# Eight of 31 convolution taps moved to ScalarE and GpSimd, and the product order and operand buffers of a seven-product FFN changed

## The chip, the cores and the metric

The kernel runs on one core of one Trainium2 chip, as one launch. The metric is the device time of that launch in microseconds. The engines are named as the profile names them: PE is TensorE, DVE is VectorE, ACT is ScalarE, POOL is GpSimd, SP is SyncE, whose queue issues most DMAs.

## What is computed

One layer of an encoder over 1024 tokens of width 1024, all in float32: a mixer of two branches, then a SwiGLU network (FFN) of width 2816, each with a residual, and a last RMS norm.

```python
h = rmsnorm(x, norm_mix)
a_val, a_gate, u, v, g_a, g_b = split(h @ w_in)          # six times 1024 columns
c = a_val * sigmoid(a_gate)
c = depthwise_conv(c, conv_w, conv_b)                    # width 31, centred, along the tokens
y_a = silu(layernorm(c, conv_ln_g, conv_ln_b)) @ w_conv_out
y_b = spatial_gating(u, v) @ w_sgu_out                   # 128x128 position mixing per chunk and group
x = x + (sigmoid(g_a + gb_a) * y_a + sigmoid(g_b + gb_b) * y_b) @ w_o
h2 = rmsnorm(x, norm_ffn)
x = x + (silu(h2 @ w_ffn_gate) * (h2 @ w_ffn_up)) @ w_ffn_down
return rmsnorm(x, norm_final)
```

## The kernel before

**Operands in two parts.** Every float32 matrix operand is split into a high part (rounded to fp32r by ACT, L84) and a low part (the rest, by DVE, L85), and a product is three matmuls: high by high, high by low, low by high. A matmul has 128 rows by 512 columns.

**Mixer.** Channels lie on partitions, tokens on the free axis, so a channel's 1024 tokens are one row. The program runs as a list of jobs of 48 matmuls, each with one 128-column block of weights: for each of eight channel blocks j a gate job (pg) and a value job (pv), from which c_j is made; between them the v products and the mixing; then eight pu jobs, then eight pairs pb and py, then eight pga jobs. The two parts of a job's weights lie in the pool tag wh with four buffers, that is two jobs' weights: the split for a job can begin when the job two places ahead of it has ended on PE, and must be done when the job just ahead of it ends.

**Convolution.** Each channel block's 31 taps are done on DVE beside those jobs: the centre tap writes conv_j with the bias (L212), the other 30 are each one scalar_tensor_tensor, conv_j = c_j shifted, times a weight per channel, plus conv_j (L218). They stand in the queue bg; pump(n) emits the next n of them after a job, and what is left is emitted after the last py job. The sum over the channel blocks (conv_sum, L396) goes to PE as conv_mean behind the first pga job.

**FFN.** After two plain rows f = 0 and 1, ten iterations take two rows of 128 columns each. The product of a 2x2 block of weights (two rows by two halves of the inputs) with a 2x2 block of activations is made by seven products in place of eight, for the gate (call g) and for the up matrix (call u). The names p1 to p7 stand here for the product of weight operand w1 to w7 with its activation operand: a product is 12 matmuls. The activation operands (y11, y21, y22, t1 to t4, four tiles each) are made once and stay in the pool act. The weight operands are made for every call by w_operands: four sums on DVE and seven splits, all into the four buffers of wh. Products land in two PSUM tiles of two banks each, pa (b1 and b2) and pb (b3), and are read by ACT or DVE between products: s1 = copy of b1 (L654), s2 (L656), s3 (L660), then the four results.

**Who sets the order.** The code gives each engine's work and the tiles; a scheduler at build time sets the order on each engine, and an engine runs its list strictly in that order. It orders a product into pa behind a read of the other bank of pa. Pools: act has 42 buffers of 4 KB per partition, tmp two, and a tile can be written when the last user of its buffer is done.

## Time and profile before

| what | value |
|---|---|
| median of 2 runs | 1554.85 us (1554.05 to 1555.65) |
| profiled execution, its own time | 1553.29 us |
| its span, first to last instruction | 1551.5 us |
| PE busy, share of the span | 1508.7 us, 97% |
| DVE busy | 925.7 us, 60% |
| ACT busy | 419.8 us, 27% |
| POOL busy | 68.0 us, 4% |
| granted TensorE clock, mean | 0.998 of full speed |

PE is the engine to explain. Matmuls overlap, so a PE that is shown as busy is not a PE at its rate: the number of matmuls in a stretch tells how near it is. Shares of the other engines are means over stages that differ much; a stage is read by its own windows.

### The profile page before, as it was taken

To read this page: it belongs to the slowest core of one execution; us is meant where nothing else is said; L and a number is where in the kernel's file an instruction comes from. 1 tells how busy PE (TensorE), PEld (TensorE's weight loads), DVE (VectorE), ACT (ScalarE), POOL (GpSimd) and SP (SyncE) were. 2 spreads that over 40 slices of the span, in tenths; PEclk is the share of its full clock that TensorE was granted. 3 is DMA by queue.
4 is the path that set the end of the run, shared out by engine and by line. 5 is a ranking of instruction groups with operands and counts; after the bars stand their busy time and mean duration, and the time that the engine had idled before them with its cause. 6 is when DMAs were issued, how large, how long until landed. Compare 5 with 4: busy or idle time off the path is not lost.

```text
span 1551.5 us, 16509 instructions
## 1 busy us (share of the span) xinstructions
PE 1508.7 (97%) x6728; PEld 1228.4 (79%) x6728; DVE 925.7 (60%) x1115; ACT 419.8 (27%) x603; POOL 68.0 (4%) x116
## 2 busy tenths in 40 slices
PE   6999999999999999999999999999999999999997
PEld 6888888888888888888888777777777777887885
DVE  5889799498999526434523755555555555444412
ACT  6220101121111115612323422222223223333301
POOL 1000100000000000110010000000000000000000
PEclk9999999999999999999999999999999999999999
DMA  4240011111222122461611212122222224663502
GB/s 191 71 137 14 10 33 41 54 42 55 62 74 81 55 96 82 138 229 41 230 64 59 95 68 67 69 68 82 82 76 74 82 86 160 220 199 103 183 1 81
DMA packets 43036, 141.73 MB, mean 91 GB/s; under 512 B 4785, under 2 KB 4785, under 8 KB 42961
## 3 DMA queue, kind: packets, MB, share of 16 engines
q1 hardware_dynamic: 32256, 101.73, 20.3%
q0 software_dynamic: 10704, 38.96, 6.9%
q8 instruction: 52, 0.85, 0.2%
q14 instruction: 24, 0.19, 0.0%
HBM read 112.36 MB, written 28.31 MB: 91 GB/s over the span
## 4 chain that ended last, share of the span: by engine, by line
PE 96%; ACT 2%; DVE 1%; issue 0%; DMA 0%; POOL 0%; POOLq 0%; SPq 0%; ACTq 0%; DVEq 0%
PE fd L494 15%; PE pa_g L640 9%; PE pa_u L640 9%; PE pga L110 6%; PE po L494 6%; PE py L110 6%; PE pb L110 6%; PE pu L110 6%; PE pco L110 6%; PE pv L110 5%; PE pg L110 5%; PE pb_g L640 4%; PE pb_u L640 3%; PE v L298 2%; PE v L300 2%; PE v L299 2%
## 5 line engine op out<-in xcount | busy, mean ns | idle before, releaser
L218 DVE SCALAR_TENSOR_TENSOR conv<-c,vec,conv 128x1021 f32<-128x1021 f32 (+14 forms) x240 | 301.1, 1272 | 4.4
L494 PE MATMUL fd<-wh_d,ff 128*128 128x512 f32 x704 | 198.9, 389 | 2.0 <-ACT ff L84 2.0
L494 PEld LDWEIGHTS fd<-wh_d,ff 128*128 128x128 f32 x704 | 132.0, 188 | 29.9 <-ACT ff L84 2.5
L84 ACT CAST wh_in<-ws_in 128x1024 fp32r<-128x1024 f32 x40 | 42.2, 1054 | 303.3 <-PE pg L110 77.5
L494 PE MATMUL fd<-wl_d,ff 128*128 128x512 f32 x352 | 118.7, 389 | 0.0
L640 PE MATMUL pa_g<-t,w_g 128*128 128x512 f32 x360 | 89.8, 398 | 0.0
L640 PE MATMUL pa_u<-t,w_u 128*128 128x512 f32 x360 | 88.6, 395 | 0.4 <-DVE s_u L660 0.4
L640 PEld LDWEIGHTS pa_g<-t,w_g 128*128 128x128 f32 x360 | 65.3, 188 | 20.7 <-ACT fa L677 3.1
L640 PEld LDWEIGHTS pa_u<-t,w_u 128*128 128x128 f32 x360 | 66.0, 188 | 18.5 <-DVE fa L688 3.0
L494 PEld LDWEIGHTS fd<-wl_d,ff 128*128 128x128 f32 x352 | 66.1, 188 | 13.8
L110 PE MATMUL pg<-hT,wh_in 128*128 128x512 f32 (+1 forms) x272 | 74.1, 383 | 2.6 <-DVE hT L181 2.0
L85 DVE TENSOR_TENSOR wl_in<-ws_in,wh_in 128x1024 fp32r<-128x1024 f32 x40 | 48.8, 1219 | 41.2 <-ACT wh_in L84 41.1
L110 PE MATMUL pv<-hT,wh_in 128*128 128x512 f32 (+1 forms) x272 | 71.0, 377 | 0.0
L110 PE MATMUL pga<-hT,wh_in 128*128 128x512 f32 x256 | 69.4, 393 | 0.0
L494 PE MATMUL po<-wh_o,mT 128*128 128x512 f32 x256 | 69.1, 390 | 0.0
L110 PE MATMUL pco<-sT,wh_co 128*128 128x512 f32 x256 | 68.4, 389 | 0.0
L110 PE MATMUL pu<-hT,wh_in 128*128 128x512 f32 x256 | 68.4, 389 | 0.0
L110 PE MATMUL pb<-hT,wh_in 128*128 128x512 f32 x256 | 68.4, 389 | 0.0
L110 PE MATMUL py<-gT,wh_so 128*128 128x512 f32 x256 | 68.4, 389 | 0.0
L85 DVE TENSOR_TENSOR wl_d<-ws_d,wh_d 128x1024 fp32r<-128x1024 f32 x32 | 39.1, 1225 | 45.9 <-ACT wh_d L84 45.8
L640 PE MATMUL pa_g<-y,w_g 128*128 128x512 f32 x240 | 61.4, 399 | 2.6 <-ACT w_g L84 2.3
L110 PEld LDWEIGHTS pg<-hT,wh_in 128*128 128x128 f32 x272 | 50.5, 188 | 14.3 <-DVE hT L181 3.3
(216 smaller groups left out, 2654.0 us busy)
## 6 DMA issues: line engine op xcount, KB each, us to landing
ws_in<-in_w_in SPq DMA_DIRECT2D x40, 512.0 KB, 3.7
ws_d<-in_w_down SPq DMA_DIRECT2D x32, 512.0 KB, 4.0
ws_g<-in_w_gate SPq DMA_DIRECT2D x22, 512.0 KB, 3.6
ws_u<-in_w_up SPq DMA_DIRECT2D x22, 512.0 KB, 4.4
ff_d<-fa POOLq DMA_DIRECT2D x22, 512.0 KB, 4.0
ffr<-ff_d SPq DMA_DIRECT2D x44, 256.0 KB, 3.7
x<-in_x SPq DMA_DIRECT2D x16, 512.0 KB, 6.5
ws_v<-in_w_v SPq DMA_DIRECT2D x8, 512.0 KB, 3.7
```

Source lines behind the costliest of these rows:

```text
L84: nc.scalar.copy(hi, src)
L85: nc.vector.tensor_sub(lo, src, hi.bitcast(F32))
L110: nc.tensor.matmul(p[:, h * H + lo_t:h * H + hi_t], wt[:, sl], a[part][h][j][:, i, lo_t:hi_t], start=(k == 0 and wt is hi and part == 0), ...
L218: nc.vector.scalar_tensor_tensor(o[:, a:b], c[:, a + d:b + d], vcol(V_CW, j * TAPS + t), o[:, a:b], ALU.mult, ALU.add)
L298: nc.tensor.matmul(p[:, i2, :], lh, whi, start=(k == 0), stop=False)
L299: nc.tensor.matmul(p[:, i2, :], lh, wlo, start=False, stop=False)
L300: nc.tensor.matmul(p[:, i2, :], ll, whi, start=False, stop=(k == KT - 1))
L494: nc.tensor.matmul(p[c], l[:, sl], r[:, c * H:(c + 1) * H], start=(start and l is lh and r is wh), stop=(stop and l is ll))
L640: nc.tensor.matmul(p, w[n][:, q, sl], a[i][:, r, :], start=(start and i == 0 and m == 0), stop=(i == 3 and m == 2), skip_group_check=True)
```

## The change

**Convolution.** Of the 30 taps beside the centre, the eight nearest to it (SIDE) leave DVE. ACT multiplies the shifted c_j by the tap's weight: the first into a tile side_j, the other seven into tiles tap_j. POOL adds those seven to side_j (L241), and DVE adds side_j to conv_j at the end (join). The side taps stand in bg between DVE's taps, one for every two.

**FFN.** The products run in the order p1, p2, p6, p5, p7, p3, p4; before, p1, p6, p2, p7, p5, p4, p3. w1 is made with the opposite sign, so that results are one difference each. The reads of PSUM between products are three copies on ACT and three differences on DVE per call, with the last result read straight from PSUM; before, one copy and five differences. The operands w3, w6 and w7 lie in the pool act, so that wh's four buffers hold w1, w2, w4 and w5 alone. The tile u moves from act to tmp.

**Memory.** The pool act has 45 buffers in place of 42, and the scratch for DMA descriptors of POOL's queue is set to 4096 bytes.

```diff
@@ -35,7 +35,7 @@
     nc = tc.nc
 
     const = ctx.enter_context(tc.tile_pool(name="const", bufs=1))
-    act = ctx.enter_context(tc.tile_pool(name="act", bufs=42))
+    act = ctx.enter_context(tc.tile_pool(name="act", bufs=45))
     tmp = ctx.enter_context(tc.tile_pool(name="tmp", bufs=2))
     wp = ctx.enter_context(tc.tile_pool(name="wp", bufs=2))
     small = ctx.enter_context(tc.tile_pool(name="small", bufs=4))
@@ -206,22 +206,49 @@
     hT = pairs()
     conv = [None] * KT
 
+    SIDE = [PAD - 1, PAD + 1, PAD - 2, PAD + 2, PAD - 3, PAD + 3, PAD - 4, PAD + 4]
+
     def queue_conv(j, c):
+        side = [None]
+
         def center():
             conv[j] = A(f"conv_{j}")
             nc.vector.tensor_scalar(conv[j], c, vcol(V_CW, j * TAPS + PAD), vcol(V_CB, j),
                                     ALU.mult, ALU.add)
 
+        def cols(t):
+            d = t - PAD
+            a, b = max(0, -d), S - max(0, d)
+            return slice(a, b), slice(a + d, b + d)
+
         def tap(t):
-            o, d = conv[j], t - PAD
-            a, b = max(0, -d), S - max(0, d)
-            nc.vector.scalar_tensor_tensor(o[:, a:b], c[:, a + d:b + d],
-                                           vcol(V_CW, j * TAPS + t), o[:, a:b],
+            to, of = cols(t)
+            o = conv[j]
+            nc.vector.scalar_tensor_tensor(o[:, to], c[:, of], vcol(V_CW, j * TAPS + t), o[:, to],
                                            ALU.mult, ALU.add)
+
+        def side_tap(n, t):
+
+            to, of = cols(t)
+            if n == 0:
+                side[0] = A(f"side_{j}")
+                nc.gpsimd.memset(side[0][:, 0:1], 0.0)
+                nc.scalar.activation(side[0][:, to], c[:, of], AF.Copy,
+                                     scale=vcol(V_CW, j * TAPS + t))
+                return
+            m = A(f"tap_{j}_{t}")
+            nc.scalar.activation(m[:, to], c[:, of], AF.Copy, scale=vcol(V_CW, j * TAPS + t))
+            nc.gpsimd.tensor_tensor(side[0][:, to], side[0][:, to], m[:, to], op=ALU.add)
+
+        def join():
+            nc.vector.tensor_add(conv[j], conv[j], side[0])
         bg.append(center)
-        for t in range(TAPS):
-            if t != PAD:
-                bg.append(lambda t=t: tap(t))
+        rest = [t for t in range(TAPS) if t != PAD and t not in SIDE]
+        for n, t in enumerate(rest):
+            if n % 2 == 0 and n // 2 < len(SIDE):
+                bg.append(lambda n=n // 2, t=SIDE[n // 2]: side_tap(n, t))
+            bg.append(lambda t=t: tap(t))
+        bg.append(join)
 
     def glu_out(j, sg, pg, pv):
         c = A(f"c_{j}")
@@ -609,6 +636,7 @@
 
     def w_operands(src, f, name):
 
+
         r0, r1 = w_raw(src[f], f"{name}{f}"), w_raw(src[f + 1], f"{name}{f + 1}")
         x11, x12, x21, x22 = r0[:, :H], r0[:, H:], r1[:, :H], r1[:, H:]
         sa, sb = two(f"sa_{name}{f}"), two(f"sb_{name}{f}")
@@ -616,20 +644,28 @@
         out = {}
 
         def put(n, s):
-            o = wp.tile([P, 2, H], F32R, tag="wh", name=f"w{n}_{name}{f}", bufs=4)
-            split(s, o[:, 0, :], o[:, 1, :])
+            if n in (6, 7, 3):
+                o = two(f"w{n}_{name}{f}", F32R)
+            else:
+                o = wp.tile([P, 2, H], F32R, tag="wh", name=f"w{n}_{name}{f}", bufs=4)
+            hi, lo = o[:, 0, :], o[:, 1, :]
+            if n == 1:
+                nc.scalar.activation(hi, s, AF.Copy, scale=-1.0)
+                nc.vector.scalar_tensor_tensor(lo, s, -1.0, hi.bitcast(F32), ALU.mult, ALU.subtract)
+            else:
+                split(s, hi, lo)
             out[n] = o
         put(1, x11)
+        put(2, x12)
         nc.vector.tensor_add(sp, x21, x22)
         nc.vector.tensor_add(sq, x11, sp)
         put(6, sq)
-        put(2, x12)
+        put(5, sp)
         nc.vector.tensor_add(sr, x11, x21)
         put(7, sr)
-        put(5, sp)
-        put(4, x22)
         nc.vector.tensor_add(sz, x12, sq)
         put(3, sz)
+        put(4, x22)
         return out
 
     def block(p, w, n, start):
@@ -647,46 +683,45 @@
 
         pa, pb = PS(f"pa_{name}", (P, 2, H)), PS(f"pb_{name}", (P, 2, H))
         b1, b2, b3 = pa[:, 0, :], pa[:, 1, :], pb[:, 0, :]
-        s12 = two(f"s12_{name}")
-        s3_ = A(f"s3_{name}", F32, (P, H))
-        s1, s2, s3 = s12[:, 0, :], s12[:, 1, :], s3_
+        s12, s5 = two(f"s12_{name}"), A(f"s5_{name}", F32, (P, H))
+        s1, s2 = s12[:, 0, :], s12[:, 1, :]
         block(b1, w, 1, True)
         nc.scalar.copy(s1, b1)
-        block(b2, w, 6, True)
-        nc.vector.tensor_sub(s2, b2, s1)
-        block(b1, w, 2, False)
-        c11(b1)
-        block(b2, w, 7, False)
-        nc.vector.tensor_sub(s3, b2, s1)
+        block(b2, w, 2, True)
+        c11(lambda o: nc.vector.tensor_sub(o, b2, s1))
+        block(b1, w, 6, False)
+        nc.scalar.copy(s2, b1)
         block(b3, w, 5, True)
-        c22(lambda o: nc.vector.tensor_sub(o, s3, b3))
-        block(b2, w, 4, False)
-        c21(lambda o: nc.vector.tensor_sub(o, b2, s1))
+        nc.scalar.copy(s5, b3)
+        block(b1, w, 7, False)
+        c22(lambda o: nc.vector.tensor_sub(o, b1, s5))
         block(b3, w, 3, False)
         c12(lambda o: nc.vector.tensor_sub(o, b3, s2))
+        block(b1, w, 4, False)
+        c21(b1)
 
     def ffn_in(f, wg, next_w):
         a = [two(f"fa_{f + n}") for n in range(2)]
 
         def gate_block(n, h):
-            def put(sub):
-                sub(a[n][:, h, :])
+            def put(add):
+                add(a[n][:, h, :])
                 nc.scalar.activation(a[n][:, h, :], a[n][:, h, :], AF.Silu)
             return put
-        blocks(wg, f"g{f}",
-               lambda b: nc.scalar.activation(a[0][:, 0, :], b, AF.Silu),
-               gate_block(1, 0), gate_block(1, 1), gate_block(0, 1))
+        blocks(wg, f"g{f}", gate_block(0, 0),
+               lambda b: nc.scalar.activation(a[1][:, 0, :], b, AF.Silu),
+               gate_block(1, 1), gate_block(0, 1))
         wu = w_operands(w_up, f, "u")
-        u = two(f"u_{f}")
+        u = T(f"u_{f}", (P, 2, H))
 
         def up_block(n, h, i):
-            def put(sub):
-                sub(u[:, i, :])
+            def put(add):
+                add(u[:, i, :])
                 nc.vector.tensor_mul(a[n][:, h, :], a[n][:, h, :], u[:, i, :])
             return put
-        blocks(wu, f"u{f}",
-               lambda b: nc.vector.tensor_mul(a[0][:, 0, :], a[0][:, 0, :], b),
-               up_block(1, 0, 0), up_block(1, 1, 1), up_block(0, 1, 0))
+        blocks(wu, f"u{f}", up_block(0, 0, 0),
+               lambda b: nc.vector.tensor_mul(a[1][:, 0, :], a[1][:, 0, :], b),
+               up_block(1, 1, 1), up_block(0, 1, 0))
         wn = next_w()
         for n in range(2):
             nc.gpsimd.dma_start(ff_d[f + n], a[n].rearrange("p a b -> p (a b)"))
@@ -811,7 +846,8 @@
     }
     arrays = {f"in_{k}": _np.ascontiguousarray(v) for k, v in arrays.items()}
 
-    nc = _bacc.Bacc("TRN2", target_bir_lowering=False, num_devices=1)
+    nc = _bacc.Bacc("TRN2", target_bir_lowering=False, num_devices=1,
+                     dynamic_dma_scratch_size=4096)
     args = [nc.dram_tensor(k, v.shape, _mybir.dt.from_np(v.dtype), kind="ExternalInput").ap()
             for k, v in arrays.items()]
     for i, (shape, dtype) in enumerate(_OUTS):
```

The order on PE is the same in both kernels up to the first of the seven-product calls. Within a call it changes. On PE, call g for rows 8 and 9, from the end of p1 on (y11, y21 and t2 are the activation operands of p1, p2 and p6; t1 with w5 is p5, which fills in), before:

```order
L640 MATMUL pa_g8_6544<-y11_3_5106,w1_g8_6515 128x512 x3
L640 MATMUL pb_g8_6545<-t1_0_5609,w5_g8_6530 128x512 x2
L640 MATMUL pa_g8_6544<-t2_0_5603,w6_g8_6520 128x512 x3
L640 MATMUL pa_g8_6544<-t2_1_5621,w6_g8_6520 128x512 x3
L640 MATMUL pa_g8_6544<-t2_2_5688,w6_g8_6520 128x512 x3
L640 MATMUL pa_g8_6544<-t2_3_5706,w6_g8_6520 128x512 x3
L640 MATMUL pb_g8_6545<-t1_0_5609,w5_g8_6530 128x512
L640 MATMUL pb_g8_6545<-t1_1_5627,w5_g8_6530 128x512 x3
L640 MATMUL pa_g8_6544<-y21_0_5181,w2_g8_6523 128x512 x3
```

and now:

```order
L676 MATMUL pa_g8_6680<-y11_3_5242,w1_g8_6651 128x512 x3
L676 MATMUL pb_g8_6681<-t1_0_5745,w5_g8_6662 128x512 x3
L676 MATMUL pb_g8_6681<-t1_1_5763,w5_g8_6662 128x512
L676 MATMUL pa_g8_6680<-y21_0_5317,w2_g8_6654 128x512 x3
L676 MATMUL pa_g8_6680<-y21_1_5321,w2_g8_6654 128x512 x3
L676 MATMUL pa_g8_6680<-y21_2_5335,w2_g8_6654 128x512 x3
L676 MATMUL pa_g8_6680<-y21_3_5339,w2_g8_6654 128x512 x3
L676 MATMUL pb_g8_6681<-t1_1_5763,w5_g8_6662 128x512 x2
L676 MATMUL pb_g8_6681<-t1_2_5830,w5_g8_6662 128x512 x2
L676 MATMUL pa_g8_6680<-t2_0_5739,w6_g8_6659 128x512 x3
```

Behind p1 stood two matmuls of p5 and then p6; now four of p5 stand there, then p2, four more of p5, then p6.

On ACT, around the same call: L84 makes high parts, s12 is the tile of s1 and s2 (and s5 holds p5), fa are the FFN's activations. Before:

```order
L84 CAST w1_g8_6515<-ws_g8_6509 128x512 [waits DMAHW2_49,DVE_49,PE_49]
L84 CAST w6_g8_6520<-sa_g8_6513 128x512 [waits DVE_49,PE_49,Activation_49]
L84 CAST w2_g8_6523<-ws_g8_6509 128x512 [waits PE_49,Activation_49]
L84 CAST w7_g8_6527<-sb_g8_6514 128x512 [waits DVE_49,PE_49,Activation_49]
L84 CAST w5_g8_6530<-sa_g8_6513 128x512 [waits PE_49,Activation_49]
L654 COPY s12_g8_6546<-pa_g8_6544 128x512
L84 CAST w4_g8_6533<-ws_g9_6511 128x512 [waits DMAHW3_49,DVE_49,PE_49]
L84 CAST w3_g8_6537<-sb_g8_6514 128x512 [waits DVE_49,PE_49,Activation_49]
L677 ACTIVATE fa_8_6542<-pa_g8_6544 128x512 [waits DMASW1_49,DVE_49]
```

and now:

```order
L84 CAST w5_g8_6662<-sa_g8_6649 128x512 [waits DVE_49,Activation_49]
L84 CAST w6_g8_6659<-sa_g8_6649 128x512 [waits DMASW0_49,DVE_49]
L84 CAST w7_g8_6666<-sb_g8_6650 128x512 [waits DVE_49]
L84 CAST w3_g8_6670<-sb_g8_6650 128x512 [waits DVE_49]
L84 CAST w4_g8_6673<-ws_g9_6647 128x512 [waits DMAHW1_49,PE_49,Activation_49]
L689 COPY s12_g8_6682<-pa_g8_6680 128x512 [waits PE_49]
L653 ACTIVATE w1_u8_6784<-ws_u8_6778 128x512 [waits DMAHW2_49,Activation_49]
L84 CAST w2_u8_6787<-ws_u8_6778 128x512 [waits PE_49,Activation_49]
L709 ACTIVATE fa_8_6678<-fa_8_6678 128x512 [waits DVE_49]
L693 COPY s12_g8_6682<-pa_g8_6680 128x512 [waits PE_49]
L695 COPY s5_g8_6683<-pb_g8_6681 128x512 [waits PE_49]
L709 ACTIVATE fa_9_6679<-fa_9_6679 128x512 [waits DVE_49]
```

All seven casts of call g8 now stand ahead of its first copy of PSUM (its w1 and w2 still earlier, in the call before), and the casts that follow are of call u8; before, five stood ahead of it, each behind the release of a wh buffer, and two behind it.

On ACT in the mixer, from the end of the job pu_6 on (wh_in32 are the weights of pb_0, wh_so0 those of py_0, side_5 and tap_5 the side taps of channel block 5). Before:

```order
L84 CAST wh_in32_2445<-ws_in32_2443 128x1024 [waits DMAHW0_49,PE_49,Activation_49]
L84 CAST gT0_0_3_2499<-mixed_6_1522 128x512 [waits DVE_49]
L84 CAST gT0_1_3_2503<-mixed_6_1522 128x512
L84 CAST wh_so0_2515<-ws_so0_2513 128x1024 [waits DMAHW1_49,PE_49,Activation_49]
L84 CAST gT0_0_3_2499<-mixed_7_1533 128x512 [waits DVE_49]
L84 CAST gT0_1_3_2503<-mixed_7_1533 128x512
L84 CAST wh_in33_2596<-ws_in33_2594 128x1024 [waits DMAHW2_49,PE_49,Activation_49]
```

and now:

```order
L84 CAST wh_in32_2525<-ws_in32_2523 128x1024 [waits DMAHW0_49,PE_49,Activation_49]
L84 CAST gT0_0_3_2579<-mixed_6_1562 128x512 [waits DVE_49,Activation_49]
L84 CAST gT0_1_3_2583<-mixed_6_1562 128x512 [waits Pool_49]
L236 ACTIVATE side_5_2655<-c_5_1827,vec_83 128x1023 [waits Pool_49]
L240 ACTIVATE tap_5_16_2733<-c_5_1827,vec_83 128x1023 [waits Activation_49]
L240 ACTIVATE tap_5_13_2738<-c_5_1827,vec_83 128x1022 [waits DVE_49]
L240 ACTIVATE tap_5_17_2743<-c_5_1827,vec_83 128x1022 [waits Pool_49]
L240 ACTIVATE tap_5_12_2805<-c_5_1827,vec_83 128x1021 [waits Pool_49]
L240 ACTIVATE tap_5_18_2810<-c_5_1827,vec_83 128x1021 [waits Pool_49]
L240 ACTIVATE tap_5_11_2872<-c_5_1827,vec_83 128x1020 [waits Pool_49]
L84 CAST wh_so0_2594<-ws_so0_2592 128x1024 [waits DMAHW1_49,PE_49]
L240 ACTIVATE tap_5_19_2877<-c_5_1827,vec_83 128x1020 [waits Pool_49]
```

Seven multiplications now stand between two casts of weights, five of them with a wait for POOL.

## Rows read from the trace of the kernel before

**Rows 1.** Two windows: PE, PEld, DVE, ACT, POOL busy us (count), clock, DMA, GB/s.

```profile
400.00:500.00 100.00, 100.00 (x443) 82.81 (x442) 99.94 (x86) 15.52 (x15) 2.37 (x5) 1.00 0.21 69
...
900.00:1000.00 100.00, 95.67 (x402) 73.22 (x401) 52.70 (x83) 28.57 (x49) 2.13 (x4) 1.00 0.22 74
```

**Rows 2.** Chain that ended last, in order of time: start, us, piece.

```profile
302.36 87.04 PE pu L110 x384
389.40 10.88 PE pb L110 x48
...
574.37 1.72 PE conv_mean L403 x4
...
880.61 2.73 PE pa_g L640 x12
...
922.64 2.51 PE pa_g L640 x11
...
964.48 2.51 PE pa_g L640 x11
...
1299.45 119.69 PE fd L494 x528
```

**Rows 3.** Timeline of call g, rows 6 and 7: start, us, instruction, idle before.

```profile
967.06 0.62 ACT L84 CAST w_g<-sa_g 128x512 fp32r<-128x512 f32 x1 [1.88 <-PE pa_g L640]
...
967.59 0.58 ACT L654 COPY s_g<-pa_g 128x512 f32<-128x512 f32 x1
...
967.73 0.30 PEld L640 LDWEIGHTS pb_g<-t,w_g 128*128 128x128 f32 x2 [1.19 <-ACT w_g L84]
...
968.30 2.95 PE L640 MATMUL pa_g<-t,w_g 128*128 128x512 f32 x12
...
971.36 0.69 DVE L656 TENSOR_TENSOR s_g<-pa_g,s_g 128x512 f32<-128x512 f32 x1 [2.95 <-PE pa_g L640]
...
972.11 3.02 PE L640 MATMUL pa_g<-y,w_g 128*128 128x512 f32 x12
...
980.18 3.02 PE L640 MATMUL pa_g<-t,w_g 128*128 128x512 f32 x12
```

**Rows 4.** Costliest groups of the page: line, operation, count, busy us, mean ns.

```profile
L218 DVE SCALAR_TENSOR_TENSOR conv<-c,vec,conv 128x1021 f32<-128x1021 f32 (+14 forms) x240 | 301.1, 1272 | 4.4
...
L84 ACT CAST wh_in<-ws_in 128x1024 fp32r<-128x1024 f32 x40 | 42.2, 1054 | 303.3 <-PE pg L110 77.5
```

**Rows 5.** Timeline of DVE in the mixer.

```profile
390.57 1.22 DVE L85 TENSOR_TENSOR wl_so<-ws_so,wh_so 128x1024 fp32r<-128x1024 f32 x1
391.71 1.29 DVE L85 TENSOR_TENSOR gT<-mixed,gT 128x512 fp32r<-128x512 f32 x2
...
424.32 10.79 DVE L218 SCALAR_TENSOR_TENSOR conv<-c,vec,conv 128x1020 f32<-128x1020 f32 x9
...
524.11 1.23 DVE L396 TENSOR_TENSOR conv_sum<-conv_sum,conv 128x1024 f32<-128x1024 f32 x1
```

**Rows 6.** Timeline of ACT, a cast of weights between two jobs.

```profile
389.03 1.06 ACT L84 CAST wh_so<-ws_so 128x1024 fp32r<-128x1024 f32 x1 [8.07 <-issue]
```

**Rows 7.** Timeline, a small POOL operation beside a tap of DVE.

```profile
181.18 1.22 DVE L218 SCALAR_TENSOR_TENSOR conv<-c,vec,conv 128x1011 f32<-128x1011 f32 x1
181.29 1.51 POOL L79 TENSOR_TENSOR rstd_v<-ms_v,nhalf 128x1 f32<-128x1 f32 x1 [10.67 <-DVE vmv L311]
```

**Rows 8.** Timeline of POOL, the same operation twice with DVE idle.

```profile
160.75 1.17 POOL L79 TENSOR_TENSOR rstd_v<-ms_v,nhalf 128x1 f32<-128x1 f32 x2 [7.78 <-DVE ms_v L78]
```

**Rows 9.** Timeline at the start: POOL beside DVE operations end to end.

```profile
8.72 2.24 DVE L173 TENSOR_SCALAR x<-x,rstd_a 128x1024 f32<-128x1024 f32 x3
...
8.87 1.31 POOL L79 TENSOR_TENSOR rstd_a<-ms_a,nhalf 128x1 f32<-128x1 f32 x1 [1.23 <-DVE ms_a L78]
```

**Rows 10.** Groups of POOL by shape.

```profile
masks.py:199 POOL TENSOR_SCALAR_AFFINE_SELECT ident<-ident 128x128 f32<-128x128 f32 x1 | 0.3, 302 | 0.0
...
L69 POOL MEMSET nhalf<- 128x8 f32 x1 | 0.1, 114 | 0.0
```

## The prediction, made before the changed kernel ran

> **What bounds the kernel now.** I read the windows first: not how busy PE is, but how many matmuls it does in 100 us. In the mixer, from 400 to 500 us, it does 443; in the FFN, from 900 to 1000 us, 402 [rows 1]. Then the chain of waits, which gives PE's rate where nothing holds it: 384 matmuls in 87.04 us, or 0.2267 us each, and a job of 48 in 10.88 us [rows 2]. The mixer's jobs follow each other at just that rate, so PE has nothing to gain there, although DVE beside it is busy 99.94 of the 100 us [rows 1]. In the FFN the seven-product calls run from 880.61 to 1299.45 us, 418.84 us for 20 calls of 84 matmuls; at PE's rate they would take 1680 x 0.2267 = 380.8 us. So 38.0 us are lost there. The loss is regular: an iteration (168 matmuls, 38.1 us at the rate) begins at 922.64 and the next at 964.48, 41.84 us later [rows 2].
>
> The timeline of one call says where. Behind p1, PE waits for the high part of w5, which ACT casts only at 967.06, since a buffer of wh came free late; the copy s1 stands behind that cast on ACT and ends at 968.17; p6 starts at 968.30 [rows 3]. The next three switches are smaller and alike: a product of 12 and four matmuls of filling need 16 x 0.2267 = 3.63 us, but the starts at 968.30 and 972.11 are 3.81 us apart, because DVE's read of PSUM (0.69 us from 971.36) ends a little after the filling does [rows 3]. So about 0.18 us at a switch with a DVE read, and about 1 us at the first switch of a call; 38.0 / 20 = 1.9 us per call.
>
> **The FFN part.** What goes: w3, w6 and w7 leave wh, so that its four buffers serve four operands, and by the order all seven casts of a call stand before its first read of PSUM. The late cast behind p1 is gone, and with it its 1 us. What stays: three switches of pa with four matmuls of filling each (p1 to p2, p2 to p6, p6 to p7); behind p7 stands all of p3, 2.7 us, which covers any read. Of the three reads one is DVE's, 0.18 us as above. Two are now copies on ACT: 0.58 us against 0.69 [rows 3], so 0.18 - 0.11 = 0.07 us each. That is 0.32 us a call and 6.4 us for 20, with perhaps 1 us more at the first call: 38.0 - 7 = 31 us gained. Bounds: if the ACT copies cost as much as DVE's reads, and one in three comes late behind a cast by half of its 0.62 us, 0.65 us a call and 25 us gained; if they cost nothing, 0.18 us a call and 34 gained. ACT gets two more copies a call and DVE two differences fewer; both have idle time there (DVE 52.70 and ACT 28.57 us busy in 100 [rows 1]). The casts that now stand in the next call's place wait for the end of p1 and p2 on ACT, ahead of the silu and the copy s2, but these wait for later products anyway. I cost the sign of w1, the move of u and the smaller scratch at nothing: POOL's stores in the FFN come 40 us apart and nothing on PE waits for them; if a store held its tile longer, w6 would be the operand to wait.
>
> **The convolution part.** It takes 64 taps of about 1.20 us from DVE (nine take 10.79 us from end to end [rows 5]) and gives it eight joins of 1.14 us: 68 us less on an engine that PE never waits for there, so no gain on the path. conv_sum ended at about 525 us and PE wanted it at 574.37 [rows 2, 5]; this slack grows. It gives ACT 64 multiplications of about 1.05 us, as its casts of the same size [rows 4], on idle time. And it gives POOL 56 additions of 128x1024 with two inputs in SBUF. What these cost decides the case.
>
> No row shows such an addition. Its length: POOL's select of 128x128 takes 0.302 us and its smallest fill 0.114 [rows 10]; eight times the first is 2.4 us, and with the fixed part taken off once per instruction, 0.11 + 8 x 0.19 = 1.6 us. DVE's own sum of that size, 1.22 us [rows 5], is the lower bound. I take 2.0 us, the middle of POOL's own two figures.
>
> [...]
>
> Does it run beside DVE? The same one-column POOL operation takes 0.585 us with DVE idle [rows 8] and 1.51 us when it is issued 0.11 us into a tap: the tap ends at 182.40, the operation at 182.80 [rows 7]. All four of these that met a tap behaved so. POOL could not read until the tap had ended. The reverse, a tap held by POOL, has no row: the bound from below is nothing, from above the whole addition. I take the whole, since the rows show one side shut out completely, not slowed.
>
> [...]
>
> Where it hurts: from the end of pu_6 to the end of py_2, seven jobs, 76.2 us of PE. By the order DVE does there 49 taps (58.8 us), 12 sums of full size (13.7), two pairs of half size (2.5) and three centre taps (about 2.2): 77 us, as full as before. In the same stretch stand 21 of the 56 additions, because ACT multiplies in bursts there, and the next casts of weights stand behind the bursts. A job's split has slack: the cast starts at 389.03, DVE's part ends at 391.79, and PE needs it at 389.40 + 10.88 = 400.28, so 8.5 us [rows 2, 5, 6]. Work on DVE and POOL together is 77 + 21 x 2.0 = 119 us; less 76.2 and 8.5, PE falls 34 us behind. With 1.22 us an addition it is 18, with 2.4 it is 43. The other 35 additions stand where DVE has idle time; there I count nothing.
>
> **The sum.** The profiled execution took 1553.3 us, 1.6 below the median of 1554.85. 1553.3 - 31 + 34 = 1556.3; carried to the median, **1558 us**. From the bounds (18 to 43, 25 to 34 gained): 1539 to 1573.
>
> **The rivals.** First, the taps are not held: POOL's additions slip into the gaps, or both run, and ACT's multiplications are early enough. For it: no row shows DVE held, and two buffers of products let ACT run ahead. Against: rows 7. Then only the FFN part counts: 1555 - 31 = 1524, with 0 to 4 us for a late cast, 1519 to 1531.
>
> Second, slower than before: POOL never gets its turn between taps. At the start of the kernel a POOL operation of 0.55 us took 1.31 us, from 8.87 to 10.18, while DVE operations of 0.75 us ran end to end; it waited through the boundary between the first two [rows 9]. If taps keep POOL out that way, an addition runs only when DVE itself waits. In that stretch DVE waits only at a split whose cast stands on ACT behind the additions, so each addition costs its 2.0 us, a multiplication of 1.05 that ACT does after it for want of a free buffer, and some 0.2 of signals: 3.25 us. 77 + 21 x 3.25 - 84.7 = 61 us, and 1554.85 - 31 + 61 = **1585 us**, 1573 to 1600. It decides against the change from 31 us on, at 1.85 us an addition: a little under what I assume for the forecast, so the sign of my forecast is weak.
>
> Third, the FFN gains little: the pool act is as full as before, and w6, w7 and w3 get their buffers only when a store or an old operand is done. By the order some of these casts wait for a store, but for one issued a whole call earlier. With 12 us gained in place of 31 and the convolution as forecast: 1577.
>
> **Chances.** The forecast case 0.47, no hold 0.25, POOL kept out 0.18, a small gain in the FFN 0.07, anything else 0.03. The range 1521 to 1586 leaves out part of the second and of the third case, not quite 2 in 10. Two per cent, 31 us, is about what a measurement of this kernel can tell from no change; the whole loss in the FFN is hardly more. Faster than 1523.8 is half of the no-hold case: 0.13. Slower than 1586 is half of the kept-out case and a few more: 0.12. Within: 0.75.
>
> **What the profile after would show.** If the FFN part is right: an iteration takes 38.7 to 39.3 us in place of 41.84, and PE does about 435 matmuls in 100 us there; weight loads wait for the c11 difference on DVE, and no longer for casts. If the convolution part is right: additions of about 2 us on POOL, taps that start late beside them, and gaps on PE between 380 and 470 us that end with wh or wl. If POOL's additions are far longer and PE waits for ACT's casts, it is the kept-out case. If conv_mean still starts near 574 us [rows 2], it is the no-hold case. The prediction is wrong if PE waits in other places: at conv_mean for the last join, or at the v products behind a full pool act.

## The result, and the profile after

The changed kernel takes **1570.95 us** (median of two runs, 1570.90 to 1570.99) against 1554.85 before: a ratio of 1.0098, with a 95% interval of 1.0076 to 1.012. It is 16 us slower where 3 us were forecast; both lie within the two per cent. The sum of the prediction has two terms, and they came out differently: the FFN gave 31.4 us (forecast 31), the convolution cost 49.8 (forecast 34).

First the windows of the kernel after, the same two as in [rows 1]:

```profile
400.00:500.00 100.00, 82.18 (x320) 65.44 (x319) 95.51 (x57) 29.59 (x29) 58.05 (x21) 0.90 0.13 42
900.00:1000.00 100.00, 100.00 (x437) 80.74 (x437) 66.03 (x102) 44.18 (x74) 2.17 (x4) 1.00 0.23 74
```

In the FFN PE does 437 matmuls in 100 us in place of 402. In the mixer it does 320 in place of 443, POOL is now busy for 58 us of the 100, DVE finishes 57 instructions in about the time that it needed for 86, and the granted clock is 0.90. That last number was 1.00 before, and nothing in the prediction had asked for it.

The chain of waits of the kernel after, at the places that answer to [rows 2]:

```profile
613.31 10.89 PE pga L110 x48
624.19 1.72 PE conv_mean L430 x4
...
919.71 10.88 PE fu L599 x48
...
1318.05 7.03 PE fd L521 x31
```

conv_mean starts at 624.19 in place of 574.37, 49.8 us later. The seven-product calls run from 930.59, where fu ends, to 1318.05: 387.5 us in place of 418.84. The stretches between and behind differ by no more than a microsecond.

Where PE waits in the mixer (waits of the kernel after from 190 to 620 us: who waits for whom, us in total, times, the longest):

```profile
PE py L110 <- DVE wl_so L85: 8.0, 3, 4.4
PE pb L110 <- DVE wl_in L85: 7.3, 2, 5.9
PE py L110 <- ACT wh_so L84: 7.3, 1, 7.3
PE pm L367 <- DVE c L255: 4.6, 1, 4.6
PE pb L110 <- ACT wh_in L84: 3.0, 1, 3.0
```

With two small ones (1.1 and 0.5) that is 31.8 us. The other 18 of the 49.8 stand in no list of waits; the timeline of PE shows them. It has the last matmuls before a wait, the wait and what comes behind it:

```profile
410.64 0.86 PE L110 MATMUL py<-gT,wh_so 128*128 128x512 f32 x3
415.87 0.77 PE L110 MATMUL py<-gT,wl_so 128*128 128x512 f32 x2 [4.36 <-DVE wl_so L85]
416.44 1.90 PE L110 MATMUL py<-gT,wh_so 128*128 128x512 f32 x4
418.14 1.05 PE L110 MATMUL py<-gT,wl_so 128*128 128x512 f32 x2
418.99 1.49 PE L110 MATMUL py<-gT,wh_so 128*128 128x512 f32 x4
420.32 0.62 PE L110 MATMUL py<-gT,wl_so 128*128 128x512 f32 x2
420.78 1.08 PE L110 MATMUL py<-gT,wh_so 128*128 128x512 f32 x4
```

PE stands for 4.36 us. Then four matmuls take 1.90 us, where four like them take 1.08 a little later: the granted clock stands at 0.50 of full speed for 3.4 us, from 416.5 us on, and comes back. Two windows of the same columns as above show it, 0.57 of full speed on average behind the wait and 1.00 from 420.8 us on:

```profile
416.00:420.00 4.00, 4.00 (x11) 3.13 (x12) 4.00 (x4) 2.25 (x3) 2.15 (x2) 0.57 0.44 131
420.80:427.00 6.20, 6.20 (x29) 5.14 (x28) 6.20 (x5) 3.18 (x4) 4.08 (x2) 1.00 0.01 3
```

So waits of this kind cost more than their own length: the five jobs of pb and py that have them, from 410.38 to 526.10 us, take 2.0 to 3.9 us more than the 10.88 of a job and their waits together.

Why DVE is late can be read from the instructions themselves (DVE's chain piece beside an addition, then POOL's timeline with one addition that meets no tap and one that does):

```profile
395.97 3.29 DVE conv L227
```

```profile
488.46 2.37 POOL L241 TENSOR_TENSOR side<-side,tap 128x1022 f32<-128x1022 f32 x1 [1.26 <-ACT tap L240]
492.08 3.24 POOL L241 TENSOR_TENSOR side<-side,tap 128x1022 f32<-128x1022 f32 x1 [1.26 <-ACT tap L240]
```

A tap that meets an addition takes 3.29 us in place of 1.27 [rows 4]: held for 2.0 us. An addition takes 2.37 us by itself and 3.24 when it is issued into a tap. They run in turn. In the page's list of costliest groups (count, busy us, mean ns) the taps' mean is 1668 ns in place of 1272, and the split's second half, wl_in, is held too, 1414 ns in place of 1219:

```profile
L227 DVE SCALAR_TENSOR_TENSOR conv<-c,vec,conv 128x1018 f32<-128x1018 f32 (+10 forms) x176 | 291.0, 1668 | 3.5
L241 POOL TENSOR_TENSOR side<-side,tap 128x1022 f32<-128x1022 f32 (+3 forms) x56 | 169.5, 3028 | 272.3 <-ACT tap L240 270.5
...
L85 DVE TENSOR_TENSOR wl_in<-ws_in,wh_in 128x1024 fp32r<-128x1024 f32 x40 | 56.6, 1414 | 57.0 <-ACT wh_in L84 57.0
```

176 taps now keep DVE busy for 291 us; 240 took 301 before. 64 taps gone have shortened DVE's work on taps by 10 us, not 77.

### The profile page after: what moved, and what is told of

It is laid out like the page before. It is cut to its first block, busy times and chain, and to the rows that moved or that the text cites. A ratio compares the mean times of both kernels' runs of the same rounds, so it can differ in the third digit from the quotient of the medians.

```text
span 1569.1 us, 16553 instructions
## 1 busy us (share of the span) xinstructions
PE 1515.0 (97%) x6728; PEld 1242.9 (79%) x6728; DVE 921.4 (59%) x1019; ACT 509.5 (32%) x707; POOL 236.3 (15%) x180
## 4 chain that ended last, share of the span: by engine, by line
PE 78%; DVE 16%; issue 3%; POOL 1%; ACT 1%; DMA 1%; POOLq 0%; SPq 0%; DVEq 0%; ACTq 0%
PE fd L521 15%; DVE conv L227 11%; PE pa_g L676 9%; PE pa_u L676 9%; PE pga L110 6%; PE po L521 6%; PE pco L110 6%; PE py L110 4%; PE pb_u L676 3%; PE pb_g L676 3%; PE pb L110 3%; PE pv L110 2%; PE pg L110 2%; DVE wl_in L85 2%; PE v L326 2%
## 5 line engine op out<-in xcount | busy, mean ns | idle before, releaser
L227 DVE SCALAR_TENSOR_TENSOR conv<-c,vec,conv 128x1018 f32<-128x1018 f32 (+10 forms) x176 | 291.0, 1668 | 3.5
L241 POOL TENSOR_TENSOR side<-side,tap 128x1022 f32<-128x1022 f32 (+3 forms) x56 | 169.5, 3028 | 272.3 <-ACT tap L240 270.5
L84 ACT CAST wh_in<-ws_in 128x1024 fp32r<-128x1024 f32 x40 | 42.0, 1050 | 221.0 <-PE pg L110 59.5
L85 DVE TENSOR_TENSOR wl_in<-ws_in,wh_in 128x1024 fp32r<-128x1024 f32 x40 | 56.6, 1414 | 57.0 <-ACT wh_in L84 57.0
L110 PE MATMUL py<-gT,wh_so 128*128 128x512 f32 x256 | 74.1, 414 | 7.3 <-ACT wh_so L84 7.3
L240 ACT ACTIVATE tap<-c,vec 128x1022 f32<-128x1022 f32 (+3 forms) x56 | 62.2, 1143 | 54.2 <-POOL side L241 49.6
```

Of the source, the lines that this page charges most:

```text
L84: nc.scalar.copy(hi, src)
L85: nc.vector.tensor_sub(lo, src, hi.bitcast(F32))
L110: nc.tensor.matmul(p[:, h * H + lo_t:h * H + hi_t], wt[:, sl], a[part][h][j][:, i, lo_t:hi_t], start=(k == 0 and wt is hi and part == 0), ...
L227: nc.vector.scalar_tensor_tensor(o[:, to], c[:, of], vcol(V_CW, j * TAPS + t), o[:, to], ALU.mult, ALU.add)
L240: nc.scalar.activation(m[:, to], c[:, of], AF.Copy, scale=vcol(V_CW, j * TAPS + t))
L241: nc.gpsimd.tensor_tensor(side[0][:, to], side[0][:, to], m[:, to], op=ALU.add)
```

## The experiments

Two theories were set against each other. **Theory A**: GpSimd's additions and VectorE's instructions with two operands in SBUF exclude each other, so that their lengths add up; all of the loss follows from that. **Theory B**: ScalarE's queue does it. The multiplications stand ahead of the casts of weights, and PE's longest wait, 7.3 us, ends with a cast. All times below are medians, and the ratios are to the kernel before on the same chip.

### The two parts apart

The FFN part alone: the changed kernel with the old queue of taps.

```diff
-    SIDE = [PAD - 1, PAD + 1, PAD - 2, PAD + 2, PAD - 3, PAD + 3, PAD - 4, PAD + 4]
...
+        for t in range(TAPS):
+            if t != PAD:
+                bg.append(lambda t=t: tap(t))
```

> The FFN part without the convolution part. Both theories say that the two parts are independent: the seven-product calls took 418.84 us before and 387.46 after, so 1554.85 - 31.4 = 1523.5 us, with the granted clock at 1.00 from 200 to 500 us and conv_mean at about 574 us again. If part of the gain of 31.4 us hung on the convolution (a fresh start of the FFN after a freer pool act), the time would lie above 1528.

Measured: 1523.19 us, ratio 0.9783 (0.9768 to 0.9797). The calls run from 882.61 to 1270.05 us, 387.4, as in the changed kernel, and PE waits nowhere in the mixer. This version beats both kernels.

The convolution part alone is the same cut from the other side: the kernel before with the side taps and the memory of the changed kernel.

```diff
+    SIDE = [PAD - 1, PAD + 1, PAD - 2, PAD + 2, PAD - 3, PAD + 3, PAD - 4, PAD + 4]
...
+        bg.append(join)
```

> The convolution part without the FFN part. If the loss of the mixer is all of the difference, po starts 49.8 us later as in the changed kernel and the time is 1554.85 + 49.8 = 1604.7 us, 1602 to 1607. If the larger pool or the smaller DMA scratch costs something by itself, more than that.

Measured: 1602.66 us, ratio 1.0292 (1.0275 to 1.0309). PE's waits in the mixer are the seven of the changed kernel, each within 0.1 us. The two parts hardly touch each other: -34 and +46 us make +12, against +15 or 16 measured for both, and the change of memory, which comes next, is in both parts and so counted twice.

And the memory alone, the pool of 45 buffers with the scratch of 4 KB:

```diff
-    act = ctx.enter_context(tc.tile_pool(name="act", bufs=42))
+    act = ctx.enter_context(tc.tile_pool(name="act", bufs=45))
...
+                     dynamic_dma_scratch_size=4096)
```

> The kernel before with the pool act of 45 buffers and the DMA scratch of 4 KB, and nothing else changed. Costed at nothing in the prediction: 1553 to 1557 us. If the smaller scratch delays GpSimd's stores, it is slower by a few microseconds.

Measured: 1553.46 us, ratio 0.9982 (0.9972 to 0.9991). It costs nothing. It seems to gain some 3 us, and the other kernels with the larger memory come out 2 to 4 us better against the kernel before than their traces say (ffn_alone by 33.8 in place of 31.4). Most of that goes with the granted clock. The trace of the kernel before is of an execution of 1553.29 us at a mean granted clock of 0.998; the later executions of the same kernel took 1553.6 to 1554.8 us at 0.998 and 1557.2 to 1558.4 at 0.995, and their medians lie 3 to 4 us above the one that was traced. At 0.998 memory_alone took 1552.0 to 1553.4 us, so that about 1 us may be left for the memory, for which no trace shows a place.

### Who holds whom: the additions moved, removed and replaced

The additions on VectorE, the products still on ScalarE:

```diff
-            nc.gpsimd.tensor_tensor(side[0][:, to], side[0][:, to], m[:, to], op=ALU.add)
+            nc.vector.tensor_add(side[0][:, to], side[0][:, to], m[:, to])
```

> The products stay on ScalarE, but the 56 additions are made by VectorE, which so has as much work as in the kernel before (64 taps of 1.2 us gone, 56 additions and 8 joins of 1.14 us come). Theory A (GpSimd's additions and VectorE's taps exclude each other, and the lengths add up): nothing is left that holds a tap, 1523 to 1530 us, taps at 1.27 us again. Theory B (ScalarE's multiplications stand ahead of the casts of weights, and PE waits for those: its longest wait, 7.3 us, ends with a cast): the loss stays for the most part, 1550 to 1571 us.

Measured: 1522.36 us, ratio 0.978 (0.9765 to 0.9794). In its groups the taps are back at 1.27 us, and an addition takes VectorE 1.21 us:

```profile
L227 DVE SCALAR_TENSOR_TENSOR conv<-c,vec,conv 128x1018 f32<-128x1018 f32 (+10 forms) x176 | 221.9, 1271 | 2.8
L241 DVE TENSOR_TENSOR side<-side,tap 128x1022 f32<-128x1022 f32 (+3 forms) x56 | 67.9, 1212 | 0.3
```

All of the loss is gone, though ScalarE has the same 64 multiplications ahead of the same casts. Theory B by itself falls. The time is that of ffn_alone (1523.19 us): so the side taps gain nothing either, since PE lost nothing in the mixer before.

The additions left out:

```diff
-            nc.gpsimd.tensor_tensor(side[0][:, to], side[0][:, to], m[:, to], op=ALU.add)
```

> The 56 additions are left out, so that the convolution lacks seven of its taps; ScalarE makes all its products, and VectorE's load is 64 us lower. Theory A: nothing on GpSimd holds VectorE, 1523 to 1524 us. Theory B: the multiplications still stand ahead of the casts, though none waits for a buffer any more: PE's waits for ScalarE of 10.3 us and what the clock adds, 1533 to 1541 us.

Measured: 1522.51 us, ratio 0.9782 (0.9768 to 0.9797), with no wait of PE in the mixer. DVE is busy for 832.6 us here and for 921.4 in the changed kernel, with the same instructions on DVE: the 56 additions hold it for 88.8 us, 1.6 each on average, since some of them, such as the three from 378.36 us on, meet no DVE instruction. With the additions on DVE it was busy for 893.3 us, at the same time for the kernel: in these two kernels, where nothing holds DVE, 61 us more or less on it change nothing.

Fills in place of the additions, which write the same tile and read nothing:

```diff
-            nc.gpsimd.tensor_tensor(side[0][:, to], side[0][:, to], m[:, to], op=ALU.add)
+            nc.gpsimd.memset(side[0][:, to], 0.0)
```

> Each of GpSimd's 56 additions is replaced by a fill of the same 128x1024 tile, which writes SBUF and reads nothing, so that the convolution lacks its eight side taps. If it is reading that excludes VectorE's taps, they take 1.27 us again and the time is that without the additions, 1522 to 1525 us. If any GpSimd instruction on SBUF holds VectorE, taps beside fills are longer by the length of a fill: if that is 1 us, 56 us of holding less 77 us of taps gone, so 1523 to 1530 in time, but taps of over 2 us in the trace.

Measured: 1522.49 us, ratio 0.9786 (0.9769 to 0.9802). From its groups and, last, its timelines of POOL and of DVE:

```profile
L241 POOL MEMSET side<- 128x1022 f32 (+3 forms) x56 | 56.4, 1007 | 201.1 <-ACT side L236 198.4
...
L227 DVE SCALAR_TENSOR_TENSOR conv<-c,vec,conv 128x1018 f32<-128x1018 f32 (+10 forms) x176 | 220.9, 1270 | 3.5
```

```profile
384.26 7.46 POOL L241 MEMSET side<- 128x1023 f32 x7 [18.22 <-ACT side L236]
```

```profile
384.11 1.65 DVE L216 TENSOR_SCALAR conv<-c,vec 128x1024 f32<-128x1024 f32 x1
385.80 7.81 DVE L227 SCALAR_TENSOR_TENSOR conv<-c,vec,conv 128x1009 f32<-128x1009 f32 x6
```

Six taps run end to end in 7.81 us while POOL makes seven fills. So it is GpSimd's reading that excludes a tap, not that GpSimd is busy. The row above the taps is a surprise: the centre tap, with one operand in SBUF, takes 1.65 us here. The eight centre taps of this run take 0.80 to 1.65 us, with a median of 1.10; in the changed kernel all eight take 0.79 to 0.81.

Copies in place of the additions, with one operand read:

```diff
-            nc.gpsimd.tensor_tensor(side[0][:, to], side[0][:, to], m[:, to], op=ALU.add)
+            nc.gpsimd.tensor_copy(side[0][:, to], m[:, to])
```

> Each of GpSimd's 56 additions is replaced by a copy of the product into the side tile, which reads one tile of SBUF and not two, so that the convolution lacks seven of its taps. If any reading GpSimd instruction shuts a tap out, some taps take 1.27 us plus the length of a copy, over 2 us, in the trace; the time would be near 1523 to 1530, since 56 copies of some 1.1 us (a fill took 1.007) are no more than the 68 us taken from VectorE. If it takes two operands from SBUF on GpSimd, all taps are 1.27 us long and the time is 1522 to 1524.

Measured: 1530.44 us, ratio 0.983 (0.9815 to 0.9845). The groups of its taps and copies, and six taps and a split's second half from its timeline beside copies:

```profile
L241 POOL COPY side<-tap 128x1022 f32<-128x1022 f32 (+3 forms) x56 | 91.2, 1628 | 315.9 <-ACT tap L240 314.5
...
L227 DVE SCALAR_TENSOR_TENSOR conv<-c,vec,conv 128x1018 f32<-128x1018 f32 (+10 forms) x176 | 243.5, 1400 | 3.5
```

```profile
384.17 11.09 DVE L227 SCALAR_TENSOR_TENSOR conv<-c,vec,conv 128x1009 f32<-128x1009 f32 x6
395.18 2.05 DVE L85 TENSOR_TENSOR wl_so<-ws_so,wh_so 128x1024 fp32r<-128x1024 f32 x1
```

A copy takes 1.03 us by itself and holds a tap too: six take 11.09 us in place of 7.81, the split's half 2.05 in place of 1.22. So a GpSimd instruction that reads one operand excludes a tap as the addition with two does; the hold is shorter, as the copy is: no tap of this run takes over 2.39 us. The time is at the upper end of what was expected, 8 us above that without additions, and here PE waits for casts on ScalarE (2.6 and 1.9 us): the copies (1628 ns) take longer than the products (about 1.15 us), ScalarE waits for a buffer, and a cast waits behind it. That is theory B's queue, but only as a follower of A.

### How many, and where

Four side taps for each convolution, 24 additions:

```diff
-    SIDE = [PAD - 1, PAD + 1, PAD - 2, PAD + 2, PAD - 3, PAD + 3, PAD - 4, PAD + 4]
+    SIDE = [PAD - 1, PAD + 1, PAD - 2, PAD + 2]
```

> Four side taps for each convolution in place of eight, so 24 additions on GpSimd in place of 56, and 32 taps gone from VectorE in place of 64. If the lengths add up over the whole convolution (theory A), VectorE and GpSimd together get 24 x 2.1 + 8 x 1.14 - 32 x 1.2 = 21 us more, against 56 x 2.1 + 9 - 77 = 50 with eight: 1523.2 + 21 = 1544 us. If the 8.5 us of slack in a job's split hide the first of it, 1536. If the loss came from a few clashes whose number doesn't follow the work, it may lie anywhere between 1523 and 1571.

Measured: 1542.01 us, ratio 0.9907 (0.9891 to 0.9924). That is 19 us above the FFN part alone, close to the 21 of the sum over the whole convolution. The next two runs show that the agreement was in part chance.

Side taps for the first four convolutions only:

```diff
+        SIDE = SIDES if j < 4 else []
```

> Side taps only for the first four of the eight convolutions; the other four as before. 28 additions of about 2.1 us, 4 joins, 32 taps of 1.2 us fewer: 25 us more for VectorE and GpSimd together. If the step of the prediction holds that additions cost nothing where VectorE has idle time (46 us of it from 130 to 400 us in the kernel before), the time is 1523 to 1528. If the lengths simply add up over the whole convolution, 1523.2 + 25 = 1548. If only the first clash is left, PE's wait of 4.6 us at 205 us and what comes with it (PE is 8 us late behind it in the changed kernel), 1531 to 1534.

Measured: 1531.17 us, ratio 0.9836 (0.9821 to 0.985). 28 additions cost 8 us, the third of the cases expected, and PE has one wait of size:

```profile
PE pm L369 <- DVE c L257: 4.6, 1, 4.6
PE pu L110 <- DVE wl_in L85: 1.1, 1, 1.1
```

The last four only:

```diff
+        SIDE = SIDES if j >= 4 else []
```

> Side taps only for the last four convolutions. Again 25 us more work. VectorE has no idle time from 400 to 500 us, so the work falls on PE's path at once, with what the lower clock adds after each wait: 1523.2 + 25 + 5 to 15 = 1553 to 1563. If the loss of the first four is carried along to this place in the changed kernel and isn't made here, 1535 to 1545.

Measured: 1565.39 us, ratio 1.0056 (1.0039 to 1.0073). 28 additions cost 42 us, more than any number expected. Its waits of PE:

```profile
PE py L110 <- DVE wl_so L85: 7.1, 3, 3.7
PE py L110 <- ACT wh_so L84: 6.3, 1, 6.3
PE pb L110 <- DVE wl_in L85: 5.9, 2, 4.7
PE pb L110 <- ACT wh_in L84: 3.9, 1, 3.9
PE pu L110 <- DVE wl_in L85: 3.2, 1, 3.2
```

That is 26.4 us; of the other 16 an estimated 14 are PE at the lower clock behind these waits, where four matmuls take 1.91 us in place of 1.07 (granted clock 0.88 from 400 to 500 us). Early and late together make 50 us, as the changed kernel's 49.8. The same number of additions costs five times as much where DVE has next to no idle time. A sum over the whole convolution, which gives 25 us for each half, is wrong; what counts is the place.

### The FFN part taken apart

The new order, with all operands in wh again, and then the old order with w3, w6 and w7 in act and the memory of the changed kernel:

```diff
-            if n in (6, 7, 3):
-                o = two(f"w{n}_{name}{f}", F32R)
...
+            o = wp.tile([P, 2, H], F32R, tag="wh", name=f"w{n}_{name}{f}", bufs=4)
```

> The FFN part with the new order of products and the three copies on ScalarE, but with all operands in the four buffers of wh again; the convolution as before. If the gain comes from the buffers (the late cast behind p1 costs about 1 us a call), some 20 us of the 31 are lost again: 1540 to 1545 us. If it is the order that frees buffers in time, 1523 to 1526.

Measured: 1543.45 us, ratio 0.9919 (0.9905 to 0.9934). The calls take 410.7 us (880.98 to 1291.66), 8 less than before. Its timelines of ACT, and then of PE, in call g:

```profile
974.06 0.62 ACT L84 CAST w_g<-ws_g 128x512 fp32r<-128x512 f32 x1 [2.48 <-PE pa_g L646]
974.58 0.58 ACT L663 COPY s_g<-pa_g 128x512 f32<-128x512 f32 x1
```

```profile
975.22 3.02 PE L646 MATMUL pa_g<-t,w_g 128*128 128x512 f32 x12 [0.79 <-ACT s_g L663]
```

The late cast has moved, as the first of the cases expected has it: it waits for p6 to release a buffer of wh, the copy s2 stands behind it on ACT, and p7 waits for the copy.

```diff
+            if n in (6, 7, 3):
+                o = two(f"w{n}_{name}{f}", F32R)
+            else:
+                o = wp.tile([P, 2, H], F32R, tag="wh", name=f"w{n}_{name}{f}", bufs=4)
```

> The old order of products, with w3, w6 and w7 in the pool act, and the memory of the changed kernel; the convolution as before. By the account of 1.9 us lost a call, about 1.0 to 1.3 at the late cast and 0.18 at each of three switches with a read by VectorE, the cast's part goes: 20 x 1.0 to 1.3 = 20 to 26 us, 1529 to 1535 us. If the buffers alone do nothing, since the casts still stand behind reads of PSUM, 1550 to 1555.

Measured: 1546.65 us, ratio 0.9938 (0.9922 to 0.9954); 412.5 us for the calls (882.49 to 1294.94), 6 less than before: between the two cases expected, nearer to nothing. PE's timeline of call g:

```profile
966.69 1.89 PE L643 MATMUL pa_u<-y,w_u 128*128 128x512 f32 x6
...
971.49 1.07 PE L643 MATMUL pa_u<-y,w_u 128*128 128x512 f32 x4
972.51 3.01 PE L643 MATMUL pa_g<-y,w_g 128*128 128x512 f32 x12
975.36 0.61 PE L643 MATMUL pa_u<-y,w_u 128*128 128x512 f32 x2
976.21 3.01 PE L643 MATMUL pa_g<-t,w_g 128*128 128x512 f32 x12 [0.23 <-ACT fa L680]
980.07 3.02 PE L643 MATMUL pa_g<-t,w_g 128*128 128x512 f32 x12 [0.85 <-DVE s_g L663]
```

No cast is late here (PE waits seven times for the low part of an operand in call u, 2.1 us in all). But the filling has changed: matmuls of the next call's p1 (pa_u) stand at the first three switches, six, four and two of them, and none is left for the fourth, where PE waits for the whole of DVE's read. Each half of the edit gives 6 to 8 us of the calls, both together 31. From these traces I take it that the buffers take the late cast away, and that the order, in which all of p3 covers the fourth switch of pa, needs less filling; no further run separates the two.

## Why the prediction was right or wrong, point by point

**What bounds the kernel** held: PE's rate in both stages, with 84 matmuls a call that lost 1.9 us each.

**The FFN part** was right in size and in mechanism. Forecast: 7 of 38.0 us stay; measured: 387.5 - 380.8 = 6.7. An iteration takes 38.7 us (969.38 to 1008.11 in the chain), and the casts are out of PE's waits, as the weight loads' waits from 880 to 1320 us show:

```profile
PEld pa_u L676 <- DVE u L691: 3.1, 10, 0.4
PEld pa_g L676 <- DVE fa L691: 3.0, 10, 0.3
PEld pa_g L676 <- ACT s_g L689: 2.0, 10, 0.2
```

Its account of where the gain comes from was incomplete: it has the cast's 1 us a call go with the buffers and the order together, and the runs show that neither gives it alone: with the order alone a late cast stands ahead of p7, with the buffers alone no cast is late, but a switch has no filling left. The sign of w1, the move of u and the memory were costed at nothing, and nothing shows of them.

**The convolution part** had the right mechanism and the wrong size: 34 forecast, 49.8 measured. Three of its inputs stood: an addition holds a tap for 2.0 us (3.29 - 1.27), which was the value taken, though by itself an addition takes 2.37; VectorE is held as GpSimd is, which no row of before had shown and the author had inferred from GpSimd's side [rows 7]; and the work hurts where DVE is full. By the runs it is GpSimd's reading that holds a tap: 3.29 us beside an addition, 1.27 beside a fill.

What failed is the size of the **term of 34 us**. By its kind: 31.8 of the 49.8 us are waits; that this is near to 34 is luck, since they are not where they were put, and 18.0 are a piece that the sum doesn't have. The measured 49.8 lies above this term's own upper bound, 43; the time lies just within the 1539 to 1573 of the bounds, because there the FFN's gain was taken at its least, 25, and it came to 31.4.

- The clock. From pb_0 at 399.50 to the end of py_3 at about 526.1 lie 126.6 us for eight jobs of 10.88, 39.6 us lost; 25.6 are waits, some 12.5 are matmuls at the lower clock behind them, 1.90 us for four in place of 1.08, and the rest is the end of the last matmul before each wait. Behind the wait at pm the 96 matmuls that are left take 13.45 us (rows below), where the 128 of before took 14.46 (last row below), so 10.85 for 96: 2.6 us more. The sum took PE's full rate as given, since the rows of before show no other. The last 1.4 us are not placed.
- "The other 35 additions stand where DVE has idle time; there I count nothing." They cost 10 us: pb_0 starts at 399.50 in place of 389.24. The idle time absorbs most of them, but at 205 us DVE works off a queue of held taps before it makes c, and the products pm wait 4.6 us behind it. early_side shows that alone, 8 us.
- The stretch. It was taken from the end of pu_6 to the end of py_2. In the trace PE loses nothing in it before 411 us and is still losing at 513, in py_3. Its 8.5 us of slack did hide the first clashes. But of the 21 additions that were put there only 15 ran before py_2 ended, at 486.2 us, where PE had lost 21.4 us; the other six ran beside pb_3 and py_3, where it lost the other 18.2. The stretch is two jobs longer at its end, with the longest wait in the second.

PE's timeline of the kernel after at pm, and, last, of the kernel before:

```profile
201.53 3.74 PE L367 MATMUL pm<-w_sp_t,vraw 128*128 128x128 f32 x32
209.83 13.45 PE L367 MATMUL pm<-w_sp_t,vraw 128*128 128x128 f32 x96 [4.57 <-DVE c L255]
```

```profile
200.85 14.46 PE L340 MATMUL pm<-w_sp_t,vraw 128*128 128x128 f32 x128
```

**The rivals.** No hold is refuted: taps of 3.29 us. POOL kept out between taps is refuted as the rule, since additions and taps run in turn (seven additions in 23.02 us from 395.03 us on), but parts of it are there: 10.3 us of the waits end with casts that stand on ACT behind products, which wait for POOL to free a buffer, and one addition waited through five taps, 8.74 us from 478.46. The longest wait, 7.3 us at py_3, ends with such a cast (509.83 us), behind four products that each waited 3.3 us for POOL. The rival's sum of 61 us rested on additions that run only when DVE waits. A small gain in the FFN is refuted.

**What the profile would show**: the iteration, the matmuls in 100 us and the weight loads' waits came as described; the gaps of PE end with wl, and two of them with wh, but at 411 to 514 us in place of 380 to 470. The wait for c at pm was not among the places named.

## What to carry to other kernels

Before work is moved from VectorE to GpSimd, look at where the instructions on both sides read. Here VectorE's taps, with two operands in SBUF, took 3.29 us in place of 1.27 beside GpSimd's additions, which read SBUF too, while its eight instructions with one operand in PSUM (mixed from pm) took 1.27 to 1.28 us, as before, although an addition ran from 210.84 to 214.22 us beside those from 211.93 us on. So little was moved: the lengths of taps and additions added up, and a tap of 1.2 us taken off VectorE came back as a hold of 2.0 us wherever the addition met a tap, 1.6 on average. An engine without idle time that feeds PE's weights is the wrong place for a queue, even though it never shows as the bound; 28 additions cost 8 us where it had gaps and 42 where it had next to none. And where PE waits for several microseconds, add what the lower clock takes behind the wait: here some 15 us behind 31.8 us of waits.

## What the runs showed of the hardware that was not expected

- Taps ran at full speed beside GpSimd's fills (1270 ns on average over the 176 of that run, 1272 in the kernel before) but not beside its copies (six in 11.09 us) or additions (3.29 us). The centre tap was the other way about: this tensor_scalar with one SBUF operand took 1.65 us beside fills (at 384.11 us), and 0.80 us in the changed kernel where an addition was issued into it (at 421.44 us). No run shows why.
- Taps and additions excluded each other both ways (3.29 us in place of 1.27, 3.24 in place of 2.37) but not always in turn. Nearly all additions follow the tap into which they are issued. One that was issued into a centre tap waited through the five taps behind it, 8.74 us, and did so at the same place in conv_alone (8.73) and late_side (8.70), as a copy did in one_read (7.41). Another addition that was issued into a centre tap, at 421.66 us, took only 2.84. Why is left open.
- Behind waits of 3.0 to 7.3 us the granted clock stood at 0.50 of full speed for 3.4 to 10.2 us at a time, which made a job 2.0 to 3.9 us longer; in the kernel before, ffn_alone, sum_on_dve and no_sum, where PE waits nowhere in the mixer, it is 1.00 from 40 to 620 us.
